# One fused transformer layer with a PEER expert stage: order of the three split matmuls, number of split buffers, and place of the extra tokens' rows

## The chip, the cores and the metric

The kernel runs on one core of a Trainium2 chip. The metric is device time in microseconds of one execution; lower is better. The engines are TensorE (PE, with its weight loads PEld), VectorE (DVE), ScalarE (ACT), GpSimd (POOL) and SyncE (SP); most transfers are issued from SP's queue, gathers from POOL's.

## The reference

One layer for 512 tokens of width 2048, in float32:

```
h = rmsnorm(x) * (1 + sc1) + sh1                      # sc, sh, g from c_act @ ada_w + ada_b
x = x + g1 * (concat(MLA attention(h), gated linear attention(h)) @ w_out)
h = rmsnorm(x) * (1 + sc2) + sh2
x = x + g2 * peer(h);   out = rmsnorm(x)

peer(h): q = h @ w_q; scores against 2 x 128 sub-keys for each of 8 heads
         top 16 of each half, top 16 of their 256 sums -> 128 experts a token, of 16384
         gate = softmax(best scores)
         act  = gelu(h . u[expert]);   y = sum(gate * act * v[expert])
```

The last part decides the time: 512 tokens times 128 experts, each with a row of u and a row of v of 2048 floats.

## The kernel before

**Split matmuls.** A float32 product is made of three faster ones. `split` (L109) casts a weight tile to a rounded part `whi` on ACT (L112) and subtracts, `wlo = raw - whi`, on DVE or POOL (L113). `mm3` (L104) then issues, for each piece of 128 rows, high weights by high data (L105), high by low (L106) and low weights by high data (L107), one right behind the other:

```
mm(o, wh, xh, start=first, stop=False)
mm(o, wh, xl, start=False, stop=False)
mm(o, wl, xh, start=False, stop=last)
```

`load_w` (L260) fetches a raw tile of 512 KB (`wraw`, a ring of three, on SP) and splits it. `whi` and `wlo` have two buffers each, in the pool `ws`.

**Two ways for the experts.** 160 tokens, 128 and 32 "extra" ones, go the sparse way: their 128 experts' rows are gathered by index on POOL (`gat`, L956), DVE takes the dot with the token's row (`h2s`, or `h2sb` for the extra tokens, L962), applies gelu and gate, and adds weighted rows of v to `acc0` or `accb` (L972). The rows h2s and h2sb are made by `hc` copies on ACT (L885), matmuls with the identity and copies out (L889), all ahead of the gate generation.

The other 352 tokens go the dense way, over all 16384 experts. `product1(j)` (L811) is h times u for 128 experts: two tiles of 24 matmuls each into one bank `p1`, then Gelu (L820) into `wt`. `gate` (L1010) multiplies `wt` with the dense gate tile `gtile` (L1017) and splits it (L1020, L1021). `product2(pair, g)` (L1025) is one tile of v, 256 experts by 512 columns: split (L1030 ACT, L1031 DVE) and 24 matmuls, the three of `mm3` in one bank before the next bank. Four column groups g share six banks `p2`; at a group's end `evacuate` adds its four banks to `xo` (L1046, DVE).

**Order.** Chunks of 4 or 6 j's run through the four groups; steps alternate: an odd step draws the next product1 (two tiles) ahead of its product2, an even step draws one step of the late modulation (`advance`, L279; DVE multiply and add L227 on a raw tile from the same ring of `wraw`). Sparse steps are strewn in between. Every engine's instructions run in a fixed order, which the tile framework's scheduler works out from the program's order and the buffers.

**Ahead of the dense stage.** After the retrieval (DVE), `NPRE` = 8 product1 are placed in the program ahead of the gate softmax (exp L839, ACT), with the low parts made on POOL. Then come slots and rows, the gate generation (L905 to L930: one-hot tiles on DVE L912, L913, L917, 704 matmuls L924, evictions `stg` on ACT L927, a transfer to DRAM), and more product1 until `RAW` = 12 beyond the `NHOST` = 8 in `xo` are stored; then product2 begins.

Of the kernel before, what the change touches and what calls it, by code (L numbers as in the profile page):

```python
# [9 lines left out]
F32 = mybir.dt.float32  # L10
F32R = mybir.dt.float32r
# [5 lines left out]
OP = mybir.AluOpType  # L17
AX = mybir.AxisListType
PSUM = bass.MemoryType.PSUM
LEFT, RIGHT = "left", "right"  # L20

P = 128
T = 512
TB = 4
D = 2048
KD = 16
# [9 lines left out]
NT = T - NA  # L36
GT = 32
# [12 lines left out]
SEQ = "A0 G0 A1 B0 G1 A2 B1 G2 A3 B2 G3 A4 B3 F8-12 A5 B4 A6 F0-4 B5 A7 B6 F4-7 B7 F7-8"  # L50
EWAIT = 2
KBLOCKS = ((0, 3), (3, 3), (6, 3), (9, 4), (13, 3))
RAW = 12
NPRE = 8
NLO = 5
NLAT = 6
LOWEST = -3.4028235e38
# [27 lines left out]
def hybrid_layer(ctx, tc, a, out):  # L85
# [13 lines left out]
    def bank(tag):  # L99
        return cur[tag][0].tile([P, 512], F32, name="b_" + tag, tag=tag)  # L100
# [3 lines left out]
    def mm3(o, wh, wl, xh, xl, first, last):  # L104
# [3 lines that stand above are left out]
# [556 lines left out]
    gate0 = keep.tile([P, P], F32, name="gate0")  # L664
    eidxb = keep.tile([P, NB], U32, name="eidxb")
    gateb = keep.tile([P, NB], F32, name="gateb")
    ws = pools.push("ws", LEFT, bufs=2)
    korder = list(range(8, 16)) + list(range(8))
    mhi, mlo = {}, {}
    for i, pieces in enumerate((((mhi, korder[:8]), (mlo, korder[:NLO])),  # L670
# [140 lines left out]
    def product1(j, lo_eng):  # L811
        b = bank("p1")
        b3 = b[:, :NT].rearrange("p (a b) -> p a b", a=NQ)
        wt = xo[:, j if j < DG else KD - NHOST + j, :] if j < NHOST else upl.tile([P, NT], F32, name="wt", tag="wt")
        for k0 in range(0, KD, 8):
            uh, ul = load_w(ws, a["u_t"][j][:, k0:k0 + 8, :], [P, 8, P], lo_eng)
            for kk in range(8):
                k = k0 + kk
                mm3(b3, uh[:, kk, :], ul[:, kk, :], h2[0][:, GA:, k, :], h2[1][:, GA:, k, :], k == 0, k == KD - 1)
        nc.scalar.activation(wt, b[:, :NT], AF.Gelu)  # L820
        raw[j] = wt

# [49 lines left out]
    nc.vector.tensor_tensor(out=slot[:, 3], in0=gres, in1=slot[:, 2], op=OP.subtract)  # L872
    pools.pop("retr")
    hsp = pools.push("h2s", RIGHT)
    h2s = hsp.tile([P, D], F32, name="h2s")
    h2sb = hsp.tile([P, D], F32, name="h2sb")
    hcp = pools.push("hcp", RIGHT, bufs=2)
    for dst, g0 in ((h2s, 0), (h2sb, GA - 1)):
        for k4 in range(4):
            b = bank("pj")  # L880
            ks = slice(k4 * 4, (k4 + 1) * 4)
            for n, src in enumerate(h2):
                hc = hcp.tile([P, 4, P // GT, GT], F32R, name="hc", tag=f"hc{n}")
                x = src[:, 0:P // GT, ks, :] if g0 == 0 else src[:, g0:g0 + 1, ks, :].broadcast_to([P, QB, 4, NB])
                nc.scalar.copy(out=hc, in_=x.rearrange("p g k t -> p k g t"))  # L885
                for j in range(4):
                    mm(b[:, j * P:(j + 1) * P], hc[:, j].rearrange("p g t -> p (g t)"), identr,
                       start=(j == 0 and n == 0), stop=(j == 3 and n == 1))
            nc.scalar.copy(out=dst[:, k4 * 512:(k4 + 1) * 512], in_=b)  # L889
    pools.pop("hcp")  # L890
    psum_done("pj", "sk", "m")
    psum(gg=6)

# [39 lines left out]


    sp = pools.push("sparse", RIGHT, bufs=3)
    acc0 = sp.tile([P, D], F32, name="acc0", bufs=1)
    accb = sp.tile([P, D], F32, name="accb", bufs=1)
    act0 = sp.tile([P, NA], F32, name="act0", bufs=1)
    wt0 = sp.tile([P, NA], F32, name="wt0", bufs=1)
    nc.gpsimd.memset(acc0, 0.0)  # L940
    nc.gpsimd.memset(accb, 0.0)

    pace = [None, None]
# [2 lines left out]
    def after(ins, name, cls):  # L946
        if name is not None:
            tc.add_manual_dep(ins.ins, name, mybir.DependencyInfo(cls, mybir.DependencyReason.DATA), reason="pace")
# [20 lines left out]

    def add(s, g):  # L970
        acc = of(s, acc0, accb)[0]
        after(nc.vector.scalar_tensor_tensor(out=acc, in0=g, scalar=wt0[:, s:s + 1], in1=acc,  # L972
                                             op0=OP.mult, op1=OP.add), pace[1], ORDER)

    LAG = 2

# [48 lines left out]
    def product2(pair, g, banks, first, last):  # L1025
        vr = ws.tile([P, 2, 512], F32, name="wraw", tag="wraw", bufs=NWRAW)
        nc.sync.dma_start(out=vr, in_=a["v_t"][pair][g])
        vh = ws.tile([P, 2, 512], F32R, name="whi", tag="whi")
        vl = ws.tile([P, 2, 512], F32R, name="wlo", tag="wlo")
        pace[0] = nc.scalar.copy(out=vh, in_=vr).ins.name  # L1030
        pace[1] = nc.vector.tensor_tensor(out=vl, in0=vr, in1=vh, op=OP.subtract).ins.name  # L1031
        for jj in range(2):
            wh, wl = wpair[pair * 2 + jj]
            for dc in range(DG):
                dsl = slice(dc * P, (dc + 1) * P)
                mm3(banks[dc][:, :NT], vh[:, jj, dsl], vl[:, jj, dsl], wh, wl, first and jj == 0, last and jj == 1)

    fresh = [True] * DG

# [25 lines left out]
        nc.sync.dma_start(out=g2d[:, c0:c0 + width], in_=acc[0:1, :])  # L1065

    def onto_x1(g):
        x1t = fin.tile([P, DG, NT], F32, name="x1t", tag="x1t")
        nc.sync.dma_start(out=x1t, in_=x1f[:, g * DG:(g + 1) * DG, :])
        for dc in range(DG):  # L1070
            n = g * DG + dc
            nc.vector.scalar_tensor_tensor(out=xo[:, n, :], in0=xo[:, n, :], scalar=G2[:, n:n + 1], in1=x1t[:, dc, :],
                                           op0=OP.mult, op1=OP.add)
# [182 lines left out]
```

## Time and profile before

| | |
|---|---|
| median of 3 runs | 3469.57 us (3462.45 to 3469.78) |
| profiled execution, its own time | 3448.51 us |
| its span in the trace | 3446.6 us |
| PE busy | 3133.1 us, 91% of the span, mean granted clock 0.967 |
| DVE busy | 2574.2 us, 75% |
| ACT busy | 1143.7 us, 33% |
| POOL busy | 980.1 us, 28% |
| DMA | 849.26 MB, mean 246 GB/s |

The shares are means over stages of different kinds; the dense stage, from about 1335 us on, is three fifths of the span. Busy time of PE counts matmuls as the trace records them; they overlap, so the sum of durations is more than the time between starts. A wait row tells who waited and for which engine's line. "PEclk" in a window is the clock that TensorE was granted, as a share of full speed.

### The profile page before, as it was taken

What the parts mean: (1) busy time and instruction counts of PE and PEld (TensorE: products, weight loads), DVE (VectorE), ACT (ScalarE), POOL (GpSimd) and SP (SyncE); (2) the same over time, 40 slices, a digit from 0 to 9 for tenths busy, and PEclk for the clock granted to TensorE, in tenths of its full rate; (3) what the DMA queues carried; (4) which work ended last, traced back from release to release, by engine and by line L of the source; (5) the groups of instructions that cost most, each with busy time, mean ns of one, the idle gap of its engine ahead of it and who ended that gap; (6) DMA issues with size and microseconds to landing.
All of it is one profiled execution on the core that took longest, in us unless ns stands there. A gap on an engine that the chain in (4) does not pass through costs nothing. (4 is left out here: it accounts for less than half of the span.)

```text
span 3446.6 us, 45915 instructions
## 1 busy us (share of the span) xinstructions
PE 3133.1 (91%) x17569; PEld 2864.9 (83%) x17569; DVE 2574.2 (75%) x3632; ACT 1143.7 (33%) x1594; POOL 980.1 (28%) x631
## 2 busy tenths in 40 slices
PE   3999999999997889989999899899989989899998
PEld 2777776787776878989999898898989889899997
DVE  8988936774897495777777777777877677777776
ACT  3333453423222674222222222222222222222333
POOL 5454511111444444222222221222222222222210
PEclk9999999999998999999999999999999999999999
DMA  7876710283222358888888888887988788787874
GB/s 225 266 249 218 254 59 19 91 288 128 92 86 80 135 214 294 319 302 316 319 315 318 302 292 305 304 302 286 332 299 305 280 302 301 288 303 291 331 278 168
DMA packets 266652, 849.26 MB, mean 246 GB/s; under 512 B 25560, under 2 KB 97912, under 8 KB 222688
## 3 DMA queue, kind: packets, MB, share of 16 engines
q1 hardware_dynamic: 219840, 510.66, 44.3%
q0 software_dynamic: 46592, 335.68, 24.6%
q8 instruction: 137, 2.24, 0.3%
q14 instruction: 83, 0.68, 0.1%
HBM read 814.74 MB, written 31.47 MB: 246 GB/s over the span
## 5 line engine op out<-in xcount | busy, mean ns | idle before, releaser
L107 PE MATMUL b_p<-h2hi,wlo 128*128 128x352 f32 x4096 | 1372.6, 336 | 164.5 <-DVE wlo L113 144.4
L105 PE MATMUL b_p<-h2hi,whi 128*128 128x352 f32 x4096 | 1362.4, 333 | 28.8 <-ACT whi L112 23.2
L106 PE MATMUL b_p<-h2lo,whi 128*128 128x352 f32 x4096 | 1355.7, 331 | 0.0
L107 PEld LDWEIGHTS b_p<-h2hi,wlo 128*128 128x128 f32 x4096 | 793.4, 194 | 192.2 <-DVE wlo L113 166.8
L105 PEld LDWEIGHTS b_p<-h2hi,whi 128*128 128x128 f32 x4096 | 794.1, 194 | 36.8 <-ACT whi L112 23.9
L106 PEld LDWEIGHTS b_p<-h2lo,whi 128*128 128x128 f32 x4096 | 793.2, 194 | 0.1
L112 ACT CAST whi<-wraw 128x1024 fp32r<-128x1024 f32 (+2 forms) x459 | 414.3, 905 | 968.2 <-PE b_p L106 440.2
L1030 ACT CAST whi<-wraw 128x1024 fp32r<-128x1024 f32 x256 | 268.8, 1050 | 918.7 <-PE b_p L106 839.1
L1031 DVE TENSOR_TENSOR wlo<-wraw,whi 128x1024 fp32r<-128x1024 f32 x256 | 313.2, 1223 | 303.8 <-ACT whi L1030 303.4
L113 POOL TENSOR_TENSOR wlo<-wraw,whi 128x512 fp32r<-128x512 f32 (+3 forms) x211 | 404.5, 1924 | 472.3 <-ACT whi L112 442.8
L956 POOL DMA_INDIRECT gat<-in_u_rows,eidx x128 | 195.4, 1527 | 614.1 <-ACT whi L1030 479.1
L956 POOL DMA_INDIRECT gat<-in_v_rows,eidx x128 | 185.6, 1450 | 612.9 <-ACT whi L1030 451.0
L227 DVE SCALAR_TENSOR_TENSOR acc<-adaw,cact,acc 128x512 f32<-128x512 f32 (+1 forms) x330 | 305.5, 948 | 26.4 <-DMA adaw<-in_ada_w 21.5
L113 DVE TENSOR_TENSOR wlo<-wraw,whi 128x1024 fp32r<-128x1024 f32 x248 | 298.2, 1217 | 31.0 <-ACT whi L112 30.2
L972 DVE SCALAR_TENSOR_TENSOR acc<-gat,wt,acc 128x2048 f32<-128x2048 f32 x128 | 300.3, 2346 | 20.1 <-DMA gat<-in_v_rows,eidx 19.9
L962 DVE SCALAR_TENSOR_TENSOR gat<-gat,h2s 128x2048 f32<-128x2048 f32 x128 | 291.7, 2286 | 25.6 <-DMA gat<-in_u_rows,eidx 25.3
L227 DVE SCALAR_TENSOR_TENSOR acc<-wraw,cact,acc 128x512 f32<-128x512 f32 x60 | 45.1, 751 | 148.4 <-DMA wraw<-in_ada_w 148.4
L1046 DVE TENSOR_TENSOR xo<-b_p,xo 128x352 f32<-128x352 f32 x236 | 106.9, 514 | 0.2 <-PE b_p L107 0.2
L107 PE MATMUL b_pj<-h2hi,wlo 128*128 128x512 f32 x256 | 102.4, 401 | 3.6 <-POOL wlo L113 3.6
L105 PE MATMUL b_pj<-h2hi,whi 128*128 128x512 f32 x256 | 102.8, 403 | 2.8 <-ACT h2hi L724 2.1
L106 PE MATMUL b_pj<-h2lo,whi 128*128 128x512 f32 x256 | 103.2, 404 | 2.0 <-DVE h2lo L725 2.0
L927 ACT ACTIVATE stg<-b_gg 128x512 f32<-128x512 f32 x88 | 87.2, 1131 | 43.3 <-PE b_gg L924 30.1
(368 smaller groups left out, 3786.0 us busy)
## 6 DMA issues: line engine op xcount, KB each, us to landing
wraw<-in_u_t SPq DMA_DIRECT2D x256, 512.0 KB, 4.7
wraw<-in_v_t SPq DMA_DIRECT2D x256, 512.0 KB, 4.8
adaw<-in_ada_w SPq DMA_DIRECT2D x224, 256.0 KB, 4.5
adaw<-in_ada_w SPq DMA_DIRECT2D x128, 192.0 KB, 3.5
gd<-stg SPq DMA_DIRECT2D x11, 2048.0 KB, 9.4
gtile<-gd SPq DMA_DIRECT2D x32, 704.0 KB, 6.6
wraw<-in_w_out SPq DMA_DIRECT2D x32, 512.0 KB, 4.5
wraw<-in_w_q SPq DMA_DIRECT2D x32, 512.0 KB, 3.6
```

The source lines that it names most:

```text
L105: mm(o, wh, xh, start=first, stop=False)
L106: mm(o, wh, xl, start=False, stop=False)
L107: mm(o, wl, xh, start=False, stop=last)
L112: nc.scalar.copy(out=hi, in_=src)
L113: (nc.vector if lo_eng == "vector" else nc.gpsimd).tensor_tensor(out=lo, in0=src, in1=hi, op=OP.subtract)
L227: nc.vector.scalar_tensor_tensor(out=acc, in0=w[:, j, :], scalar=cact[:, k:k + 1], in1=acc, op0=OP.mult, op1=OP.add)
L956: ins = nc.gpsimd.indirect_dma_start(out=g, out_offset=None, in_=a[table], in_offset=bass.IndirectOffsetOnAxis(ap=idx[:, c:c + 1], axis=0))
L962: after(nc.vector.scalar_tensor_tensor(out=g, in0=g, scalar=1.0, in1=of(s, h2s, h2sb)[0], op0=OP.mult, op1=OP.mult, accum_out=act0[:, s:s ...
L972: after(nc.vector.scalar_tensor_tensor(out=acc, in0=g, scalar=wt0[:, s:s + 1], in1=acc, op0=OP.mult, op1=OP.add), pace[1], ORDER)
L1030: pace[0] = nc.scalar.copy(out=vh, in_=vr).ins.name
L1031: pace[1] = nc.vector.tensor_tensor(out=vl, in0=vr, in1=vh, op=OP.subtract).ins.name
L1046: nc.vector.tensor_tensor(out=o, in0=banks[dc][:, :NT], in1=o, op=OP.add)
```

## The change

1. In product1 and product2 the matmuls of a tile are written in another order: first all 16 with the high weights, then the 8 with the low weights.
2. The pool `ws` gets three buffers instead of two for `whi` and `wlo`; `wraw` stays at three.
3. `RAW` goes from 12 to 13 and `NPRE` from 8 to 11, so three more product1 stand in the program ahead of the gate softmax.
4. The pool of the `hc` tiles is gone; they take turns in `whi` and `wlo`. The rows of the extra tokens, h2sb, are made ahead of the gate generation, the rows h2s after it, in banks of `p2`.
5. `acc0` is the tile h2sb, free after the extra tokens' dots; its zeroing is dropped, and the first addition is a multiplication that writes.
6. `x1t` at the end takes turns with `gtile`.

```
-RAW = 12
-NPRE = 8
+RAW = 13
+NPRE = 11
...
-    ws = pools.push("ws", LEFT, bufs=2)
+    ws = pools.push("ws", LEFT, bufs=3)
...
             for kk in range(8):
-                k = k0 + kk
-                mm3(b3, uh[:, kk, :], ul[:, kk, :], h2[0][:, GA:, k, :], h2[1][:, GA:, k, :], k == 0, k == KD - 1)
+                for x in h2:
+                    mm(b3, uh[:, kk, :], x[:, GA:, k0 + kk, :], start=k0 + kk == 0 and x is h2[0], stop=False)
+            for kk in range(8):
+                mm(b3, ul[:, kk, :], h2[0][:, GA:, k0 + kk, :], start=False, stop=k0 + kk == KD - 1)
...
-    h2s = hsp.tile([P, D], F32, name="h2s")
     h2sb = hsp.tile([P, D], F32, name="h2sb")
-    hcp = pools.push("hcp", RIGHT, bufs=2)
-    for dst, g0 in ((h2s, 0), (h2sb, GA - 1)):
+
+    def to_rows(dst, g0, ps):
         for k4 in range(4):
-            b = bank("pj")
+            b = bank(ps)
...
-                hc = hcp.tile([P, 4, P // GT, GT], F32R, name="hc", tag=f"hc{n}")
+                hc = ws.tile([P, 4, P // GT, GT], F32R, name="hc", tag=("whi", "wlo")[n])
...
-    pools.pop("hcp")
+    to_rows(h2sb, GA - 1, "pj")
     psum_done("pj", "sk", "m")
...
-    acc0 = sp.tile([P, D], F32, name="acc0", bufs=1)
+    acc0 = h2sb
+    h2s = sp.tile([P, D], F32, name="h2s", bufs=1)
+    to_rows(h2s, 0, "p2")
...
-    nc.gpsimd.memset(acc0, 0.0)
...
+        if s == 0:
+            ins = nc.vector.tensor_scalar(out=acc, in0=g, scalar1=wt0[:, s:s + 1], scalar2=None, op0=OP.mult)
...
-        for jj in range(2):
-            wh, wl = wpair[pair * 2 + jj]
-            for dc in range(DG):
-                dsl = slice(dc * P, (dc + 1) * P)
-                mm3(banks[dc][:, :NT], vh[:, jj, dsl], vl[:, jj, dsl], wh, wl, first and jj == 0, last and jj == 1)
+        for part in (vh, vl):
+            for jj in range(2):
+                for dc in range(DG):
+                    for x in wpair[pair * 2 + jj][:2 if part is vh else 1]:
+                        mm(banks[dc][:, :NT], part[:, jj, dc * P:(dc + 1) * P], x,
+                           start=first and jj == 0 and part is vh and x is wpair[pair * 2 + jj][0],
+                           stop=last and jj == 1 and part is vl)
...
-        x1t = fin.tile([P, DG, NT], F32, name="x1t", tag="x1t")
+        x1t = sp.tile([P, DG, NT], F32, name="x1t", tag="gtile", bufs=2)
```

The change moves instructions in every engine's order. Three places follow, each of before and then of the changed kernel. Line numbers of the changed kernel are up to 8 higher: product2's cast and subtraction are L1036 and L1037, the four additions L1054.

DVE at the end of a column group behind which an even step follows, with the modulation (L227); L113 are the low parts of product1 tiles, L962 or L964 the dots, L1017 or L1023 the gate multiplication. Before:

```order
L1031 TENSOR_TENSOR wlo_15534<-wraw_15531,whi_15533 128x1024
L962 SCALAR_TENSOR_TENSOR gat_15492,act0_10963<-gat_15492,h2s_9568 128x2048
L1046 TENSOR_TENSOR xo_7121<-b_p2_15389,xo_7121 128x352
L1046 TENSOR_TENSOR xo_7121<-b_p2_15390,xo_7121 128x352
L1046 TENSOR_TENSOR xo_7121<-b_p2_15391,xo_7121 128x352
L1046 TENSOR_TENSOR xo_7121<-b_p2_15392,xo_7121 128x352
L113 TENSOR_TENSOR wlo_15574<-wraw_15571,whi_15573 128x1024
L113 TENSOR_TENSOR wlo_15604<-wraw_15601,whi_15603 128x1024
L1017 TENSOR_TENSOR wt_15430<-wt_15430,gtile_15817 128x352
L227 SCALAR_TENSOR_TENSOR acc_14971<-wraw_15679,cact_87,acc_14971 128x512
```

And with the change:

```order
L964 SCALAR_TENSOR_TENSOR gat_15582,act0_11147<-gat_15582,h2s_11089 128x2048
L113 TENSOR_TENSOR wlo_15631<-wraw_15628,whi_15630 128x1024
L1023 TENSOR_TENSOR wt_15487<-wt_15487,gtile_15874 128x352
L113 TENSOR_TENSOR wlo_15661<-wraw_15658,whi_15660 128x1024
L227 SCALAR_TENSOR_TENSOR acc_15028<-wraw_15736,cact_87,acc_15028 128x512
L1054 TENSOR_TENSOR xo_7121<-b_p2_15446,xo_7121 128x352
L1054 TENSOR_TENSOR xo_7121<-b_p2_15447,xo_7121 128x352
L1054 TENSOR_TENSOR xo_7121<-b_p2_15448,xo_7121 128x352
L1054 TENSOR_TENSOR xo_7121<-b_p2_15449,xo_7121 128x352
L1037 TENSOR_TENSOR wlo_15698<-wraw_15695,whi_15697 128x1024
```

The low parts of two product1 tiles, the gate and the modulation have moved from behind the four additions to ahead of them.

DVE at the end of a group behind which product2 follows at once, of the next group. Before:

```order
L1031 TENSOR_TENSOR wlo_15399<-wraw_15396,whi_15398 128x1024
L962 SCALAR_TENSOR_TENSOR gat_15349,act0_10963<-gat_15349,h2s_9568 128x2048
L1046 TENSOR_TENSOR xo_7121<-b_p2_15147,xo_7121 128x352
L1046 TENSOR_TENSOR xo_7121<-b_p2_15148,xo_7121 128x352
L1046 TENSOR_TENSOR xo_7121<-b_p2_15149,xo_7121 128x352
L1046 TENSOR_TENSOR xo_7121<-b_p2_15150,xo_7121 128x352
```

And with the change:

```order
L1037 TENSOR_TENSOR wlo_15456<-wraw_15453,whi_15455 128x1024
L964 SCALAR_TENSOR_TENSOR gat_15406,act0_11147<-gat_15406,h2s_11089 128x2048
L964 SCALAR_TENSOR_TENSOR gat_15439,act0_11147<-gat_15439,h2s_11089 128x2048
L113 TENSOR_TENSOR wlo_15491<-wraw_15488,whi_15490 128x1024
L1023 TENSOR_TENSOR wt_15344<-wt_15344,gtile_15874 128x352
L1054 TENSOR_TENSOR xo_7121<-b_p2_15204,xo_7121 128x352
```

A second dot, a product1 tile's low part and a gate multiplication now stand between product2's low part and the additions.

ACT from the last rows ahead of the gate generation into it (`stg` is the eviction of one generation bank, `hc` the copies for the token rows, L112 the casts of product1's tiles). Before:

```order
L889 COPY h2sb<-b_pj 128x512 x2
L112 CAST whi<-wraw 128x1024
L927 ACTIVATE stg<-b_gg 128x4x128 x2
L112 CAST whi<-wraw 128x1024
L927 ACTIVATE stg<-b_gg 128x4x128 x2
L820 ACTIVATE wt<-b_p_10967 128x352
L927 ACTIVATE stg<-b_gg 128x4x128 x6
L112 CAST whi<-wraw 128x1024
```

And with the change:

```order
L886 COPY hc<-h2lo 128x512
L928 ACTIVATE stg<-b_gg 128x4x128 x88
L886 COPY hc<-h2hi 128x512
L886 COPY hc<-h2lo 128x512
L112 CAST whi<-wraw 128x1024 x3
L890 COPY h2s<-b_p_11090 128x512
```

All 88 evictions now stand in a row, and product1's casts, which were between them, behind them and behind the first `hc` copies for h2s. Further ahead in ACT's order the exp of the gate softmax stands behind two casts after the first Gelu, where it stood behind one.

## Rows read from the trace of the kernel before

**Rows 1.** Windows by stage: length, busy time of each engine (instructions), clock, DMA.

```profile
core 0: us, PE busy (x) PEld busy (x) DVE busy (x) ACT busy (x) POOL busy (x), PEclk, DMA share, GB/s
1070.00:1093.00 23.00, 0.03 (x1) 0.03 (x1) 22.90 (x106) 3.39 (x5) 0.00 (x0) 0.55 0.00 0
1162.00:1306.00 144.00, 118.86 (x1072) 103.35 (x1071) 128.31 (x167) 101.02 (x110) 66.88 (x16) 0.92 0.54 204
1335.00:2690.00 1355.00, 1249.63 (x7337) 1221.04 (x7338) 1016.60 (x1012) 387.88 (x480) 313.84 (x217) 0.97 0.85 308
2690.00:3300.00 610.00, 561.87 (x3328) 553.49 (x3328) 442.45 (x425) 173.30 (x210) 147.91 (x98) 0.97 0.81 300
1335.00:3397.00 2062.00, 1906.13 (x11251) 1868.41 (x11252) 1536.03 (x1523) 595.02 (x730) 472.86 (x321) 0.97 0.83 303
```

**Rows 2.** Windows of 20 us in the dense stage.

```profile
2980.00:3000.00 20.00, 16.28 (x88) 15.98 (x87) 13.61 (x15) 4.02 (x5) 4.21 (x3) 0.85 0.88 314
3060.00:3080.00 20.00, 20.00 (x126) 20.00 (x125) 13.81 (x12) 6.30 (x9) 5.28 (x3) 1.00 0.78 293
2760.00:2780.00 20.00, 16.86 (x105) 16.57 (x103) 16.31 (x19) 5.61 (x6) 4.53 (x3) 0.98 0.98 365
```

**Rows 3.** PE's groups by line, 1335:3397: busy us, mean ns, idle before, releasers.

```profile
L107 PE MATMUL b_p<-h2hi,wlo 128*128 128x352 f32 x3735 | 1245.6, 334 | 152.7 <-DVE wlo L113 144.4 <-DVE wlo L1031 5.4 <-POOL wlo L113 2.8
L105 PE MATMUL b_p<-h2hi,whi 128*128 128x352 f32 x3734 | 1237.5, 332 | 5.6 <-DVE xo L1046 5.4
```

**Rows 4.** Waits in the dense stage: us in total, times, longest.

```profile
PE b_p L107 <- DVE wlo L113: 144.4, 77, 4.4
```

**Rows 5.** Timeline 1902 to 1909, one end of a group: start, length.

```profile
1902.28 2.35 DVE L972 SCALAR_TENSOR_TENSOR acc<-gat,wt,acc 128x2048 f32<-128x2048 f32 x1 [0.41 <-DMA gat<-in_v_rows,eidx]
...
1904.17 1.05 ACT L112 CAST whi<-wraw 128x1024 fp32r<-128x1024 f32 x1 [1.04 <-PE b_p L106]
...
1904.55 1.81 DVE L1046 TENSOR_TENSOR xo<-b_p,xo 128x352 f32<-128x352 f32 x4
1906.27 2.35 DVE L113 TENSOR_TENSOR wlo<-wraw,whi 128x1024 fp32r<-128x1024 f32 x2
...
1907.54 0.43 PE L107 MATMUL b_p<-h2hi,wlo 128*128 128x352 f32 x1 [2.92 <-DVE wlo L113]
```

**Rows 6.** Waits of DVE in 1340 to 3390.

```profile
DVE acc L227 <- DMA wraw<-in_ada_w: 148.4, 58, 4.8
...
DVE gat L962 <- DMA gat<-in_u_rows,eidx: 25.3, 22, 2.6
```

**Rows 7.** DMA issues in 1340 to 3390: KB each, median us to landing.

```profile
wraw<-in_u_t SPq DMA_DIRECT2D x216, 512.0 KB, 4.8
...
wraw<-in_ada_w SPq DMA_DIRECT2D x64, 256.0 KB, 5.2
```

**Rows 8.** Waits of the whole program around the gate softmax.

```profile
ACT gates L839 <- DVE gates L838: 25.4, 1, 25.4
PE b_p L105 <- ACT whi L112: 23.2, 1, 23.2
```

**Rows 9.** Window of the gate generation, product1's matmuls alone: PE, PEld, DVE, ACT.

```profile
1162.00:1306.00 144.00, 87.13 (x368) 63.02 (x367) 0.00 (x0) 4.01 (x8) 0.92 0.54 204
```

**Rows 10.** Timelines of DVE and POOL in the gate generation.

```profile
1178.77 0.68 DVE L912 TENSOR_TENSOR o<-iota,slot 128x1024 f16<-128x1024 f16 x1
1179.37 1.28 DVE L917 TENSOR_TENSOR o<-o,slot 128x1024 f16<-128x1024 f16 x2
...
1208.33 2.87 DVE L912 TENSOR_TENSOR o<-iota,slot 128x1024 f16<-128x1024 f16 x1
...
1206.23 4.42 POOL L113 TENSOR_TENSOR wlo<-wraw,whi 128x1024 fp32r<-128x1024 f32 x1 [6.80 <-PE b_gg L924]
```

**Rows 11.** Groups of the page and by line: busy us, mean ns, idle before.

```profile
L927 ACT ACTIVATE stg<-b_gg 128x512 f32<-128x512 f32 x88 | 87.2, 1131 | 43.3 <-PE b_gg L924 30.1
...
L693 PE MATMUL b_o<-mixpart,whi 128*128 128x512 f32 x256 | 64.9, 393 | 0.0
```

More of the change, by code (lines that the diff above doesn't have):

```diff
@@ L971, in add @@
         acc = of(s, acc0, accb)[0]
-        after(nc.vector.scalar_tensor_tensor(out=acc, in0=g, scalar=wt0[:, s:s + 1], in1=acc,
-                                             op0=OP.mult, op1=OP.add), pace[1], ORDER)
+        if s == 0:
+            ins = nc.vector.tensor_scalar(out=acc, in0=g, scalar1=wt0[:, s:s + 1], scalar2=None, op0=OP.mult)
+        else:
+            ins = nc.vector.scalar_tensor_tensor(out=acc, in0=g, scalar=wt0[:, s:s + 1], in1=acc,
+                                                 op0=OP.mult, op1=OP.add)
+        after(ins, pace[1], ORDER)
     LAG = 2
```

## The prediction

> **What bounds the kernel now.** I read the windows by stage first. The dense expert stage, 1335 to 3397, is 2062 of 3446.6 us; in it PE is busy 1906 us at a granted clock of 0.97, DVE 1536, DMA 0.83 [rows 1]. So PE is the bound there and nothing else is full. Next, what PE's pace would be unhindered. A quiet window of 20 us, 3060 to 3080, has 126 matmuls at clock 1.00 [rows 2], 0.159 us each; I take 0.160. A matmul's own 0.33 us [rows 3] is no pace, since two overlap. The stage's 11,251 matmuls at 0.160 us would take 1800 us, so 262 us are lost.
>
> The groups of PE show where: 152.7 us idle ahead of the matmul with the weights' low part, 144.4 of it on DVE's subtraction L113, the low part of a product1 tile [rows 3], in 77 waits of up to 4.4 us [rows 4]. The other 100 us are mostly time at half clock: a disturbed window, 2980 to 3000, has 88 matmuls at clock 0.85 [rows 2], 38 fewer than the quiet one, and the granted clock falls after the longer waits.
>
> The timeline at 1904 shows why [rows 5]. When a group of product2 ends, DVE adds its four banks to the result (L1046, 1.81 us) and only then makes the low parts (2.35 us for two). PE meets the tile's first low part at its third matmul, 0.32 us in, and stands 2.92 us.
>
> **The change part by part.** The profiled execution took 3448.5 us, 0.6% less than the median of 3469.6; I sum against the former and carry the difference to the latter. I count in chunks of 24 tiles (576 matmuls, 92.2 us at 0.160). In 1335 to 2690, where the modulation (L227) still runs, 7337 matmuls in 1355 us [rows 1] make 12.74 chunks of 106.4 us; in 2690 to 3300, 3328 in 610 us make 5.78 of 105.6.
>
> *Low parts last, third buffer pair.* PE now reaches a tile's first low part after 16 matmuls, 2.6 us, instead of 2. The third whi/wlo pair lets DVE make the next product1 tile's low part ahead of the evacuation; the order of DVE's instructions shows that at both kinds of group end. Together these cover the 2.92 us of the timeline, and waits of 1.88 us on average (144.4/77). So the L113 wait and the half-clock time go, but not down to PE's pace, because of what is late next: DVE. In the first part DVE is busy 1016.6 of 1355 us [rows 1], 79.8 us a chunk. It also stands on data: L227 waits 148.4 us in 58 times for its own DMA, 2.56 each [rows 6], and that stays, since its wraw slot is freed by DVE itself a few instructions earlier and the transfer needs 5.2 us to land [rows 7]. Over 12.74 chunks that is 11.6 us each; waits for gathered rows (25.3 in all for the dot, [rows 6], and about as much for the add) are 2.6 over the 19.3 chunks of the stage. DVE thus needs 94.0 us a chunk, PE 92.2. Neither can get far ahead of the other, so what holds one up still holds up the other. I leave half of today's 14.2 us above PE's floor and take 99: 12.74 x (106.4 - 99) = 94 us gained. The ends: 92.2 (DVE's waits hidden after all) gives 181, 106.4 gives 0. In the second part DVE needs 442.45/610 x 105.6 = 76.6 us a chunk and PE binds alone; I leave 3.3 us above the floor for the bank waits below: 5.78 x (105.6 - 95.5) = 58 us, ends 77 and 0. Sum 152.
>
> *Evacuation later.* Its price is what the change adds: the four additions now stand behind the next product1 tile's low part (1.2 us), the gate multiplication and, at one kind of end, the modulation's wait. Queued behind them is product2's fifth matmul, which needs a freed bank: a group holds 4 of 6. The row of today is 5.4 us in all (L105 on DVE L1046, [rows 3]). From below it costs nothing, since DVE gets there earlier and one or two product1 tiles of 3.84 us run first at one kind of end; from above see the last rival. The 3.3 us a chunk (three ends, 1.1 us each) is nearer to the row.
>
> *Product2's low parts* now go from bank to bank at every matmul, where three in a row stayed in one. The quiet window has a bank change at every third matmul, 126 in 20 us at clock 1.00 [rows 2]: no room for a cost, so I take none. The Trainium skill's "TensorE: Matmul & The Clock Gate", section "HAM oscillation", reports a bf16 kernel whose cycling through PSUM banks idled the engine often enough for the clock to swing; it speaks against this edit, the quiet window here against the rule. By the row the term is 0, by the rule it would cost the 328 us of (d).
>
> *Gate softmax later, three more product1 tiles ahead of it.* Today ACT stands 25.4 us at the exp for DVE's gates, and PE waits 23.2 us behind it for a cast [rows 8]; in 1070 to 1093 PE is idle [rows 1]. In ACT's new order the exp comes after two casts behind the first Gelu, not one. So one more product1 tile half (24 matmuls, 3.8 us) fits in; most of the hole stays, as the other tiles' casts are still behind the exp. I count PE as resuming at 1093 with 8 tiles to go: 8 x 48 x 0.160 = 61.4, till 1154.
>
> *Rows of h2s after the gate generation, hc from the whi/wlo buffers.* This is where the change loses. The order shows 88 stg evictions in a row on ACT: the hc copies for h2s wait for PSUM that is free only after the generation, and as they take turns in whi/wlo, product1's casts queue behind them. Today 368 product1 matmuls run in 1162 to 1306 beside the generation [rows 9], 59 us at 0.160. After: the extra tokens' rows and slots take about 6 us, till 1161. The generation alone is bound by DVE: 176 instructions. Undisturbed they start 0.60 us apart; beside a POOL subtraction of 4.42 us one took 2.87 [rows 10]. With POOL's subtractions gone I take 176 x 0.60 = 106 us plus 3 to start, till 1270; ACT's 88 x 1.13 = 99 us [rows 11] fits beside. Ends: 106, or 144 as now [rows 1]. Then rows of h2s, 4 us, and the other 10 tiles of 21: 480 x 0.160 = 76.8, till 1351. Today product2 starts at 1335 with 20 tiles done, one fewer (7.7 us). So 16 - 8 = +8 us, ends +8 and +46.
>
> *The rest.* In PE's new order the last 16 matmuls of the output projection's first heads (L693), which filled gaps of the attention, stand behind it: at most 16 x 0.39 us [rows 11] = 6.3, at least 0; I take 3. The dropped memset, the shared acc0 and the first addition as a plain multiplication (2.3 us of DVE either way) and x1t from gtile's buffers move no bound: nothing for them.
>
> **Sum:** -94 - 58 + 8 + 3 = -141 us; 3448.5 gives 3307 for a profiled execution, and 3469.6 gives **3329 us** for the median.
>
> **The rivals.**
> (a) *DVE's waits are hidden too.* With DVE ahead, L227's transfer could land while PE works off tiles that are ready. For it: in the new order the low parts of two product1 tiles are made ahead of L227. Against it: the transfer is issued only when DVE frees its slot, and 94.0 is above 92.2. Then PE's floor holds: 12.74 x 14.2 + 5.78 x 13.4 = 258 gained, less 11: 3223; band 3223 to 3290.
> (b) *The ring of three wraw slots binds.* It stays at three, with five loads for four tiles in the first part. A slot is held 4.8 us for landing [rows 7], 1.05 for the cast, 1.2 for the subtraction, and what DVE does ahead: one dot (2.35) gives 9.4, an evacuation more 11.2. Over 3 slots, times 5/4, times 24 tiles this is 94 to 112 us a chunk; the middle, 103, gains 43. If the second part also gets half, 29, less 11, the time is 3409; band 3375 to 3440. For it: DMA stands at 0.83 and would rise to 0.89; a window with 365 GB/s is at DMA 0.98 with 105 matmuls only [rows 2]. Against it: ACT's casts wait mostly for PE today, not for DMA.
> (c) *Evacuations hold PE (slower).* At a group end on an odd step product2 follows at once, and covers only its first 4 matmuls, 0.64 us. DVE stands ahead of the banks with one more dot (2.35), a low part (1.2) and a gate (0.5, by its size one of the four additions): 4.1 us. At the other kind of end it is the modulation's 2.56. At full price, 32 x 4.1 + 31 x 2.56 = 210 us over 63 ends: 3539. It makes the kernel slower from 141/63 = 2.2 us a group end on. Against it: each stall of PE lets DVE catch up, and today's banks wait 5.4 us in all.
> (d) *Bank changes cost clock (slower).* If product2's low parts ran at half clock: 256 x 8 x 0.160 = 328 us more, 3657. The quiet window speaks against it. The Trainium skill's rule named above would make this the outcome.
> (e) *The edits don't reach the order,* and what pays is eaten by the generation at 144 us and the longer product1 tail: within 0.2% of 3470.
>
> **How the numbers follow.** Forecast, 3290 to 3375: 0.55. (a) 0.13, (b) 0.16, a smaller gain still, 3440 to 3461: 0.04. (e) 0.04. Slower 0.08: (c) 0.07, (d) 0.01. A measurement of this kernel can tell about 0.2% from no change. Faster 0.55 + 0.13 + 0.16 + 0.04 = 0.88. The range 3240 to 3440 leaves out some 0.04 of (a) below, and the smaller gain, (e) and the slower cases, 0.16, above.
>
> **What would show it.** Right: PE's wait on DVE's product1 low parts falls from 144 us to under 40; the dense stage's granted clock rises to 0.99; a chunk takes 99 us in the first part and 95.5 later; L227 still waits about 2.5 us each time; in the generation no product1 matmul stands beside it, its DVE instructions last under 0.7 us, and product2 starts near 1351. Wrong: product2's high matmuls waiting on DVE's evacuation for over 100 us (c); ACT's casts waiting for wraw's DMA for more than today (b); no DVE-bound stretch, chunks at 93 (a); a clock near 0.5 in product2's low parts (d).

## The result: 2.6% faster, two thirds of the forecast gain

The changed kernel takes 3380.1 us (median of 4 runs, 3365.5 to 3386.0) against 3469.7 before; the ratio is 0.974, 95% interval 0.971 to 0.978. The forecast was 3329, within 3240 to 3440. The measured time is within that range, but 5 us above the band that the forecast itself got, 3290 to 3375, and in that of rival (b), 3375 to 3440. The two profiled executions differ by less than the medians, 3381.0 against 3446.6 us of span, since that of before lay 21 us below its median and that of after 3 above.

First the windows by stage of the changed kernel (length, busy time and instructions of each engine, clock, DMA share, GB/s), to be read beside [rows 1]:

```profile
core 0: us, PE busy (x) PEld busy (x) DVE busy (x) ACT busy (x) POOL busy (x), PEclk, DMA share, GB/s
1181.00:1288.00 107.00, 75.00 (x690) 63.08 (x688) 100.85 (x166) 81.38 (x86) 0.00 (x0) 0.65 0.47 197
1370.00:2690.00 1320.00, 1219.53 (x7294) 1202.88 (x7292) 1006.49 (x1000) 378.61 (x475) 361.97 (x215) 0.96 0.87 313
2690.00:3250.00 560.00, 553.05 (x3400) 549.68 (x3400) 455.40 (x440) 179.34 (x217) 149.97 (x100) 1.00 0.92 337
```

A chunk of 576 matmuls now takes 1320 x 576/7294 = 104.2 us while the late modulation runs (before 106.4) and 560 x 576/3400 = 94.9 us after it (before 105.6). The second part is at PE's pace, clock 1.00. The first has hardly moved, at clock 0.96.

Next the waits of 1340 to 3330 (total us, times, longest), to be read beside [rows 3, 4, 6]:

```profile
ACT whi L1036 <- DMA wraw<-in_v_t: 521.6, 104, 12.5
...
ACT whi L112 <- DMA wraw<-in_u_t: 182.4, 90, 4.8
DVE acc L227 <- DMA wraw<-in_ada_w: 158.0, 50, 6.2
...
PE b_p L1042 <- DVE xo L1054: 86.3, 19, 7.0
...
PE b_p L821 <- DVE wlo L113: 0.9, 1, 0.9
```

Of PE's 144.4 us behind product1's low parts, 0.9 are left (one wait). In their place PE waits 86.3 us for the banks that the four additions free. And ACT's casts, which waited for PE before, now wait for wraw's transfers: 704 us in all, where it was 115. The rows of before, in the same stretch:

```profile
ACT whi L1030 <- PE b_p L106: 795.5, 208, 10.1
ACT whi L112 <- PE b_p L106: 411.2, 189, 4.6
...
ACT whi L112 <- DMA wraw<-in_u_t: 68.6, 18, 5.5
...
ACT whi L1030 <- DMA wraw<-in_v_t: 46.8, 14, 4.7
```

Where the bank waits come from is to be seen at 1473 to 1498, a stretch that recurs about once a chunk (timeline of ACT, DVE, PE and SP's queue: start, length):

```profile
1480.62 0.33 SPq L1033 DMA_DIRECT2D wraw<-in_v_t  x1
1481.62 0.75 DVE L227 SCALAR_TENSOR_TENSOR acc<-wraw,cact,acc 128x512 f32<-128x512 f32 x1 [1.03 <-DMA wraw<-in_ada_w]
1482.40 0.33 SPq L262 DMA_DIRECT2D wraw<-in_u_t  x1
...
1488.31 1.04 ACT L1036 CAST whi<-wraw 128x1024 fp32r<-128x1024 f32 x1 [8.71 <-DMA wraw<-in_v_t]
1489.39 1.23 DVE L1037 TENSOR_TENSOR wlo<-wraw,whi 128x1024 fp32r<-128x1024 f32 x1 [3.18 <-ACT whi L1036]
1490.53 4.73 DVE L977 SCALAR_TENSOR_TENSOR accb<-gat,wt,accb 128x2048 f32<-128x2048 f32 x2
1490.64 0.33 SPq L1033 DMA_DIRECT2D wraw<-in_v_t  x1
...
1495.18 1.22 DVE L113 TENSOR_TENSOR wlo<-wraw,whi 128x1024 fp32r<-128x1024 f32 x1
1496.32 0.52 DVE L1023 TENSOR_TENSOR wt<-wt,gtile 128x352 f32<-128x352 f32 x1
1496.75 1.81 DVE L1054 TENSOR_TENSOR xo<-b_p,xo 128x352 f32<-128x352 f32 x4
1497.32 0.66 PE L1042 MATMUL b_p<-h2hi,whi 128*128 128x352 f32 x1 [6.99 <-DVE xo L1054]
```

A load is issued when DVE has finished with a slot: 1482.40 at the end of L227, 1490.64 at the end of L1037. The tile issued at 1480.62 is cast at 1488.31, 7.7 us later. DVE waits for that cast, then runs two sparse additions, a low part and a gate, and only then adds the four banks. PE stands 6.99 us. DVE's steps are the ones that rival (c) named, with one sparse step more. That they are late because the load was is so far only read from this stretch; the run with four slots below tests it.

### The profile page after: what moved, and what is told of

It reads as the page before. It is cut to its first block, busy times and chain, and to the rows that moved or that the text cites. A ratio compares the mean times of both kernels' runs of the same rounds, so it can differ in the third digit from the quotient of the medians.

```text
span 3381.0 us, 46005 instructions
## 1 busy us (share of the span) xinstructions
PE 3111.1 (92%) x17569; PEld 2862.1 (85%) x17569; DVE 2552.5 (75%) x3630; ACT 1138.3 (34%) x1594; POOL 999.7 (30%) x632
## 5 line engine op out<-in xcount | busy, mean ns | idle before, releaser
L1042 PE MATMUL b_p<-h2hi,whi 128*128 128x352 f32 x2048 | 675.6, 332 | 105.5 <-DVE xo L1054 86.3
L112 ACT CAST whi<-wraw 128x1024 fp32r<-128x1024 f32 (+2 forms) x459 | 413.7, 904 | 886.9 <-DMA wraw<-in_u_t 196.6
L819 PE MATMUL b_p<-h2hi,whi 128*128 128x352 f32 x2048 | 671.0, 328 | 21.8 <-ACT xo L822 21.4
L1042 PE MATMUL b_p<-h2lo,whi 128*128 128x352 f32 x2048 | 668.8, 329 | 0.0
L819 PE MATMUL b_p<-h2lo,whi 128*128 128x352 f32 x2048 | 667.3, 326 | 0.0
L1036 ACT CAST whi<-wraw 128x1024 fp32r<-128x1024 f32 x256 | 268.7, 1050 | 967.2 <-DMA wraw<-in_v_t 521.6
L113 POOL TENSOR_TENSOR wlo<-wraw,whi 128x512 fp32r<-128x512 f32 (+3 forms) x213 | 378.3, 1784 | 524.9 <-ACT whi L112 352.9
L1042 PEld LDWEIGHTS b_p<-h2hi,whi 128*128 128x128 f32 x2048 | 395.9, 193 | 120.2 <-DVE xo L1054 92.7
L1037 DVE TENSOR_TENSOR wlo<-wraw,whi 128x1024 fp32r<-128x1024 f32 x256 | 312.7, 1223 | 198.9 <-ACT whi L1036 153.5
L819 PEld LDWEIGHTS b_p<-h2hi,whi 128*128 128x128 f32 x2048 | 386.7, 189 | 22.7 <-ACT xo L822 21.7
L1042 PEld LDWEIGHTS b_p<-h2lo,whi 128*128 128x128 f32 x2048 | 397.1, 194 | 0.0
L819 PEld LDWEIGHTS b_p<-h2lo,whi 128*128 128x128 f32 x2048 | 386.6, 189 | 0.1
L1042 PE MATMUL b_p<-h2hi,wlo 128*128 128x352 f32 x2048 | 376.8, 326 | 1.2 <-DVE wlo L1037 0.6
L821 PE MATMUL b_p<-h2hi,wlo 128*128 128x352 f32 x2048 | 376.0, 326 | 1.6 <-DVE wlo L113 0.9
L958 POOL DMA_INDIRECT gat<-in_u_rows,eidx x128 | 211.6, 1654 | 547.3 <-ACT whi L1036 329.5
L958 POOL DMA_INDIRECT gat<-in_v_rows,eidx x128 | 204.8, 1600 | 554.4 <-ACT whi L1036 363.3
L1042 PEld LDWEIGHTS b_p<-h2hi,wlo 128*128 128x128 f32 x2048 | 340.7, 191 | 3.0 <-DVE wlo L1037 2.9
L821 PEld LDWEIGHTS b_p<-h2hi,wlo 128*128 128x128 f32 x2048 | 340.1, 188 | 2.5 <-DVE wlo L113 1.6
L113 DVE TENSOR_TENSOR wlo<-wraw,whi 128x1024 fp32r<-128x1024 f32 x246 | 300.0, 1220 | 45.2 <-ACT whi L112 41.5
L227 DVE SCALAR_TENSOR_TENSOR acc<-adaw,cact,acc 128x512 f32<-128x512 f32 (+1 forms) x330 | 310.7, 964 | 21.5 <-DMA adaw<-in_ada_w 16.8
L977 DVE SCALAR_TENSOR_TENSOR h2sb<-gat,wt,h2sb 128x2048 f32<-128x2048 f32 x127 | 298.1, 2347 | 12.6 <-DMA gat<-in_v_rows,eidx 11.8
L964 DVE SCALAR_TENSOR_TENSOR gat<-gat,h2s 128x2048 f32<-128x2048 f32 x128 | 290.8, 2286 | 17.8 <-DMA gat<-in_u_rows,eidx 16.2
```

Source lines behind the costliest of these rows:

```text
L112: nc.scalar.copy(out=hi, in_=src)
L113: (nc.vector if lo_eng == "vector" else nc.gpsimd).tensor_tensor(out=lo, in0=src, in1=hi, op=OP.subtract)
L227: nc.vector.scalar_tensor_tensor(out=acc, in0=w[:, j, :], scalar=cact[:, k:k + 1], in1=acc, op0=OP.mult, op1=OP.add)
L819: mm(b3, uh[:, kk, :], x[:, GA:, k0 + kk, :], start=k0 + kk == 0 and x is h2[0], stop=False)
L821: mm(b3, ul[:, kk, :], h2[0][:, GA:, k0 + kk, :], start=False, stop=k0 + kk == KD - 1)
L958: ins = nc.gpsimd.indirect_dma_start(out=g, out_offset=None, in_=a[table], in_offset=bass.IndirectOffsetOnAxis(ap=idx[:, c:c + 1], axis=0))
```

## The experiments

The ratio of each row is to runs of before on the same chip in the same session (before: 3458 to 3467 us there). A chunk is 576 x length / PE's matmuls in the windows 1400 to 2700 (the modulation runs) and 2700 to 3200 (it is over). The windows are fixed, so in a faster kernel the modulation ends inside the first: its last step at L227 stands at 2644 in the changed kernel, but at 2511 in four_wraw, 2440 in ada_own_slot and 2390 in ada_two_slots.

| kernel | median us | ratio to before (95%) | chunk, first part | chunk, second part |
|---|---|---|---|---|
| before | 3469.7 | 1 | 106.9 | 106.4 |
| changed | 3380.1 | 0.974 (0.971 to 0.978) | 104.6 | 93.9 |
| two_buffers | 3389.1 | 0.979 (0.976 to 0.982) | 104.9 | 94.4 |
| old_order_three | 3394.9 | 0.982 (0.979 to 0.985) | 106.0 | 93.9 |
| before_four_wraw | 3436.0 | 0.995 (0.993 to 0.997) | 105.4 | 105.0 |
| ada_own_slot | 3318.2 | 0.958 (0.955 to 0.961) | 98.8 | 94.6 |
| ada_two_slots | 3303.0 | 0.953 (0.949 to 0.956) | 97.2 | 94.5 |
| no_late_modulation | 3268.8 | 0.944 (0.941 to 0.947) | 95.8 | 93.2 |
| four_wraw | 3272.7 | 0.946 (0.943 to 0.949) | 95.8 | 93.4 |
| old_order_four | 3290.4 | 0.952 (0.949 to 0.955) | 97.1 | 93.3 |
| rows_own_buffer | 3374.1 | 0.973 (0.971 to 0.976) | 106.6 | 93.4 |
| four_wraw_rows | 3283.2 | 0.951 (0.947 to 0.954) | 98.4 | 93.9 |
| two_pairs_five_wraw | 3375.2 | 0.977 (0.974 to 0.981) | 107.1 | 93.1 |
| additions_first | 3427.5 | 0.990 (0.987 to 0.993) | 104.3 | 103.4 |

**Which half of the change brought the gain?** The order without the third pair, and the third pair without the order.

```
-    ws = pools.push("ws", LEFT, bufs=3)
+    ws = pools.push("ws", LEFT, bufs=2)
```

is two_buffers; old_order_three puts the lines with `mm3` of before back into product1 and product2 and leaves the rest as changed.

> The changed kernel with two whi/wlo buffers instead of three: the new order of the matmuls without the third pair. In DVE's order the four additions then stand ahead of the next product1's low part again at one kind of group end. Theory: the order alone takes the waits for low parts away (2.6 us of cover), and the third pair does little or even costs, since it is what puts the additions late: 3350 to 3385, and PE's 7 us waits for the additions shrink. Rival: the third pair is needed to make low parts ahead, and without it waits of 1 to 2 us for low parts return at 77 places, with their time at half clock: 3420 to 3470.

> The changed kernel with the three matmuls of each piece in a row again, as before; three pairs of buffers and all else as changed: the third pair without the new order. Theory (the order does it, the pair adds little): PE's waits for the low parts of product1 stay above 80 us, and 22 us of later start of product2 remain: 3440 to 3490, no faster than before. Rival (the pair lets DVE make low parts ahead of the additions, and this is the gain): waits under 40 us, 3390 to 3410.

Either alone brings the second part to 94 us a chunk. Alone they are worth 2.1% and 1.8%, together 2.6%: they take away the same waits. For two_buffers the time is 4 us above the band of its theory and far from that of its rival; PE's waits for the additions shrank, to 35.1 us. The theory for old_order_three fell, and its rival was right. PE's waits in it (1370 to 3250):

```profile
PE b_p L105 <- DVE xo L1050: 46.1, 12, 4.2
PE b_p L107 <- DVE wlo L113: 32.3, 25, 4.2
PE b_p L107 <- DVE wlo L1035: 18.7, 21, 2.2
```

The waits for product1's low parts are 32.3 us with the old order of the matmuls, where before has 140.2 in that stretch, since DVE makes the low part ahead of the additions. Neither alone nor both move the first part: 104.6 to 106.0 beside 106.9. No run takes the other parts of the change alone, save the place of the rows (below).

**What holds the first part?** Four runs take away what the modulation adds, or give it room.

In ada_own_slot, with RAW 12 (ada_two_slots has bufs=2 and RAW 11):

```
-            return ws.tile([P, 512], F32, name="wraw", tag="wraw", bufs=NWRAW)
+            return sp.tile([P, 512], F32, name="adaw2", tag="adaw2", bufs=1)
```

In four_wraw:

```
-NWRAW = 3
+NWRAW = 4
...
-RAW = 13
+RAW = 10
```

In no_late_modulation:

```
-        for k0 in range(0, KD, kn):
+        for k0 in range(0, 1 if pool is ws else KD, kn):
```

> The changed kernel, but the late modulation's tiles come from a buffer of their own (one, 2 KB a partition) instead of the ring of three wraw slots; RAW 12 instead of 13 to make room. Theory R (the ring of wraw slots, with five loads for four tiles, is what binds while the modulation runs): the chunk of 576 matmuls there falls from 104.3 us to 95 or 96, as in the later part; over 12.7 chunks that is 105 to 118 us, so about 3270. Rival E (once a chunk the four additions stand behind two sparse additions, a low part and a gate on DVE, and that holds PE 7 us whatever the ring does): chunks stay at 104, time 3370 to 3390. Rival D (DVE's own load binds): 99 a chunk, about 3313.

> The changed kernel with 15 of 16 pieces of the late modulation (the last of the six sections) left out, transfers and DVE work both; the output is then not the reference's. It bounds from below what the modulation costs. Theory R: the chunk in the first part falls to 95, as in the second, the 7 us waits of PE for the four additions go: 12.7 x 9.3 = 118 less, about 3262. Rival E: chunks at 102 to 104 with a 7 us wait once a chunk, about 3370.

> As the run with one buffer of its own for the late modulation, but with two (RAW 11 to make room). With one, L227 still waited 88.8 us for its transfer, up to 8.0 at a time, with the four additions queued behind it (PE's waits for them up to 9.8). Theory: the transfer is issued too late because it shares SP's queue with loads that wait for wraw slots; with two buffers it is issued a step earlier, the waits of L227 fall under 25 us, PE's long waits for the additions go, a chunk of the first part takes 95 or 96: 3275 to 3295. Rival: DVE's load in the first part is what is left (99 a chunk): 3318 within 10.

> The changed kernel with a ring of four wraw slots instead of three, the modulation's tiles still in it (RAW 10 to make room). If it is the number of slots that binds, five loads for four tiles now have a third more slots: chunks of the first part at 95 to 98, 3275 to 3310, ACT's waits for wraw's transfers far shorter. If it is only that L227's transfer starts late, behind DVE's own low parts, chunks fall to 99 or 100 only: about 3325. If neither, 3380.

With 15 of 16 pieces of the modulation left out the first part runs at 95.8 us a chunk; with four slots and the modulation in, at the same 95.8. In 1440 to 2390, where the modulation runs in every kernel that has it, it is 96.7 and 96.4, beside 104.1 with the change, 99.3 in ada_own_slot and 98.2 in ada_two_slots. So neither DVE's work nor the traffic of the modulation is what costs, but the slots: five loads for four tiles in a ring of three. The windows of four_wraw, and its waits in 1370 to 3250:

```profile
1400.00:2700.00 1300.00, 1277.17 (x7815) 1265.92 (x7814) 1081.11 (x1071) 410.81 (x497) 330.99 (x230) 0.99 0.93 341
2700.00:3200.00 500.00, 498.69 (x3084) 497.50 (x3083) 407.73 (x407) 165.06 (x199) 107.48 (x78) 1.00 0.89 325
```

```profile
PE b_p L1042 <- DVE xo L1054: 24.1, 13, 5.7
...
ACT whi L1036 <- DMA wraw<-in_v_t: 93.4, 24, 7.1
ACT whi L112 <- DMA wraw<-in_u_t: 39.2, 14, 5.4
```

DMA moves 341 GB/s there, where it moved 313: bandwidth was not the limit. ACT's waits for wraw fall from about 700 to 133 us, and PE's bank waits from 86 to 24, though in DVE's order the additions still stand behind two sparse steps, a low part and a gate or a modulation step (these two have changed places). That settles the bank waits as a consequence of late loads. `RAW` was lowered for room in these runs, and no run lowers it alone; but no_late_modulation keeps 13 and comes to the same chunk, and before_four_wraw (below), with 11 for 12, moves little. A slot of its own for the modulation brings less. Its 98.8 us a chunk and 3318 us are what its rival D (DVE's own load binds) had said, 99 and 3313; but in four_wraw DVE has the same work a chunk, 79.7 us against 79.3, and a chunk takes 95.8, so DVE's load is not what bound. What the trace of ada_own_slot shows is that DVE meets its transfer at L227 before it has landed, with the additions behind it. Waits of ada_own_slot, then of ada_two_slots (1370 to 3250):

```profile
PE b_p L1042 <- DVE xo L1054: 54.9, 16, 9.8
...
DVE acc L227 <- DMA adaw<-in_ada_w: 88.8, 33, 8.0
```

```profile
PE b_p L1042 <- DVE xo L1054: 43.0, 14, 12.3
...
DVE acc L227 <- DMA adaw<-in_ada_w: 31.7, 13, 9.6
```

The second buffer took 57 us of waits at L227 but only 15 us of time; the expectation of 3275 to 3295 was missed by 8 us, and PE's long waits for the additions did not go.

**Was the ring the bound before, too?** One slot more on the kernel before (with x1t in gtile's buffers and RAW 11 for room).

```
-NWRAW = 3
+NWRAW = 4
```

> The kernel before with one thing changed: a ring of four wraw slots instead of three (to make room RAW 11 instead of 12, and x1t in gtile's buffers as in the change). If before was held only by the low parts that DVE makes behind the four additions, the slot more does nothing: the second part stays at 105.6 us a chunk, PE waits over 100 us for low parts, 3440 to 3470. If the ring already held the first part before, that part falls to 97 to 100 and the second stays: 12.7 x 7 = 89 less, about 3380.

It brings 0.5%, 4 us more than the first theory allowed, and neither part moves by more than 1.5 us a chunk. The reason stands in PE's first row of waits (1370 to 3250): the waits for low parts are all there. DVE's wait at L227 is nearly gone, 13.3 us where it was 148.4, and that alone gave almost nothing.

```profile
PE b_p L107 <- DVE wlo L113: 139.3, 78, 5.1
...
DVE acc L227 <- DMA wraw<-in_ada_w: 13.3, 8, 4.2
```

So before, low parts held both parts. The change took them away, and in the first part the ring of slots stood right behind, 2 us a chunk lower.

**Is the order worth more once the ring does not bind?** Four slots and three pairs as above, with the `mm3` lines of before.

> The run with four wraw slots (3273 us), with the three matmuls of each piece in a row again as before; three pairs of buffers. It asks what the new order is worth once the ring does not bind. If little, as with three slots (15 us): 3280 to 3300. If the ring hid its worth in the first part: PE's waits for low parts of 50 us and more there, with half-clock time, 3320 to 3360.

Its 3290 against 3273 with the new order: 0.6%, the intervals do not overlap. Low parts cost 22.4 us of waits in it, 14 times. It is as little as with three slots.

**Slots instead of pairs.** Hc in gathered rows' buffers (below), and

```
-NWRAW = 3
+NWRAW = 5
...
-    ws = pools.push("ws", LEFT, bufs=3)
+    ws = pools.push("ws", LEFT, bufs=2)
```

> The same space spent otherwise: two whi/wlo pairs, five wraw slots, RAW 13, hc copies of h2s in gathered rows' buffers, the new order of the matmuls. If slots of wraw are worth more than a third pair at any count: 3235 to 3250. If four slots are enough and the third pair then counts (two pairs cost 9 us with three slots): 3255 to 3275.

Both expectations fell: 3375, and a chunk of 107.1 in the first part. Five slots with two pairs are hardly better than three with two (3389); four slots with three pairs are 107 us better than three with three. Casts no longer wait for transfers but for PE and DVE to free a pair, and DVE for the modulation (1400 to 2700):

```profile
ACT whi L1039 <- PE b_p L819: 369.8, 126, 5.8
ACT whi L112 <- PE b_p L1045: 356.4, 118, 15.3
...
DVE acc L227 <- DMA wraw<-in_ada_w: 266.3, 55, 10.4
...
PE b_p L1045 <- DVE xo L1057: 68.5, 12, 10.8
ACT whi L112 <- DVE wlo L1040: 56.9, 13, 8.2
```

A tile can be ahead only if it has both a slot and a pair. Why L227 waits 266 us in this kernel, with more slots than any other, can be read from a stretch of its timeline (DVE and SP's queue):

```profile
2041.30 1.26 DVE L1040 TENSOR_TENSOR wlo<-wraw,whi 128x1024 fp32r<-128x1024 f32 x1 [0.94 <-ACT whi L1039]
...
2042.49 2.34 DVE L980 SCALAR_TENSOR_TENSOR h2sb<-gat,wt,h2sb 128x2048 f32<-128x2048 f32 x1
2042.59 0.33 SPq L221 DMA_DIRECT2D wraw<-in_ada_w  x1
...
2049.61 0.75 DVE L227 SCALAR_TENSOR_TENSOR acc<-wraw,cact,acc 128x512 f32<-128x512 f32 x1 [4.79 <-DMA wraw<-in_ada_w]
```

The modulation's load is issued when a low part has freed a slot, and in DVE's order only one sparse addition stands between that and L227. In four_wraw two low parts of product1 tiles stand between as well (2012 to 2019, where L227 does not wait). That this order comes from the missing pair was not tested.

**The four additions first.** DVE's order with the additions ahead of the next product1's low part and of the step's sparse work.

In `split` the low part is ordered behind the last addition, and after `evacuate` the sparse work is:

```
+        if lo_eng == "vector" and emptied[0] is not None:
+            tc.add_manual_dep(sub.ins, emptied[0], mybir.DependencyInfo(mybir.DependencyClass.NoSync, mybir.DependencyReason.DATA), reason="pace")
...
+                emptied[0] = nc.vector.tensor_tensor(out=o, in0=banks[dc][:, :NT], in1=o, op=OP.add).ins.name
...
                 evacuate(g, banks)
+                if emptied[0] is not None:
+                    pace[1] = emptied[0]
+                sparse_some(PER2)
```

> The changed kernel, but in DVE's order the four additions at a group's end stand ahead of the next product1's low part and of the sparse work of that step. Rival E: PE's waits for the additions (86 us) fall under 20, with the half-clock time behind them, and the time to 3290 to 3320. Theory R: the additions were only late because the ring was late; PE waits for product2's cast or low part instead, chunks stay at 101 to 104: 3350 to 3380.

Neither: it is 1.6% slower than the changed kernel, and loses in the second part, 103.4 instead of 93.9. Two rows of its waits (1370 to 3250):

```profile
DVE xo L1058 <- PE b_p L1046: 119.0, 36, 6.2
...
ACT whi L112 <- DMA wraw<-in_u_t: 350.6, 164, 7.4
```

DVE now stands at the additions until PE has finished the group, and the low parts behind them, which free wraw's slots, come late: casts of u tiles wait 350.6 us instead of 182.4. With three slots the late additions of the changed kernel are the better order; with four this was not tried.

**The empty gate generation.** hc of h2s in the gathered rows' buffers, so that product1's casts do not queue behind it; then the same with four slots.

```
-                hc = ws.tile([P, 4, P // GT, GT], F32R, name="hc", tag=("whi", "wlo")[n])
+                if ps == "pj":
+                    hc = ws.tile([P, 4, P // GT, GT], F32R, name="hc", tag=("whi", "wlo")[n])
+                else:
+                    hc = sp.tile([P, D], F32R, name="hc", tag="gat")[:, :512].rearrange("p (k g t) -> p k g t", k=4, t=GT)
```

> The changed kernel, but the hc copies for the rows of h2s take buffers of the gathered rows instead of whi/wlo, so that product1's casts no longer queue behind them; in ACT's order product1 then stands between the evictions of the gate generation again. If the empty generation is what costs the 22 us by which product2 starts later than before (1363 against 1341 at equal matmul counts), then product1's matmuls run beside the generation, which gets longer by POOL's subtractions (107 to about 140 us), and product2 starts 15 to 20 us earlier: about 3362. Rival: what the filled generation gains, its lengthening gives back: 3380 within 7.

> Four wraw slots (RAW 11) and the hc copies of h2s in gathered rows' buffers, so that product1 fills the gate generation. With three slots the 21 us that the rows' own buffer gained ahead of product2 were lost again in the first part, where chunks took 106 instead of 104. If the ring took them back, they stay now: 3273 - 21, about 3252. If the filled generation costs them elsewhere, 3273 within 7.

In the generation product1's matmuls are back; window 1181 to 1288 of rows_own_buffer, beside the first window of after above:

```profile
1181.00:1288.00 107.00, 89.29 (x817) 78.16 (x815) 103.75 (x134) 76.83 (x85) 56.78 (x11) 0.92 0.56 212
```

DVE makes 134 instead of 166 instructions in it, PE 817 instead of 690 matmuls. Product2 starts at 1342.9 instead of 1370.9; 7 of the 28 us lie ahead of product1 already. So the first half of the theory held, 21 us, but the end comes hardly earlier: 3374 is within the interval of the changed kernel, as the rival had it, and 3283 is 10 us above four_wraw, where neither expectation put it. The first part's chunk is 2.0 us longer with three slots and 2.6 with four, 25 and 32 us over 12.4 chunks (four_wraw_rows has `RAW` 11, four_wraw 10). That it was the ring which took the gain back is refuted by the second run. What does, stays open.

## Why the prediction was right in sign and range, and 51 us short

That the time lies within the range is owed to the room that the range left for rival (b): the forecast's own mechanism holds for the second part of the dense stage, that of (b) for the first.

- **The bound, right.** Low parts held PE, and their waits are gone, 144.4 us to 0.9. The half-clock time went in the second part, clock 1.00; in the first the bank waits took their place, clock 0.96. So the dense stage's 0.99 that the prediction named did not come: 0.97 in 1340 to 3330.
- **The second part, right.** 58 us forecast (95.5 a chunk), (105.6 - 94.9) x 5.78 = 62 measured.
- **The first part, the step that failed.** 94 us forecast (99 a chunk), (106.4 - 104.2) x 12.7 = 28 measured. The step passed the bound from PE to DVE at 94.0 us a chunk. DVE's own sum was right: 1006.5 us busy and 158 at L227 over 12.66 chunks are 92.0, and the gathers add about 2. But DVE was not what came late next. The ring of three slots was, as rival (b) had it: 103 a chunk there, 104.2 measured, and four slots give 95.8. Rival (b) was given 0.16 because ACT's casts waited for PE, not for DMA, in the trace of before. That argument does not hold, and the sign that the prediction named for (b), more of ACT's waits for wraw's transfers, came, 115 us to 704: while PE stands for something else, the transfers have time to land, and the row says nothing of what they will do at PE's new pace. Its own working, 9.4 to 11.2 us a slot, was the better evidence.
- **L227's wait stays, right,** and is longer: 158.0/50 = 3.2 us each instead of 2.56.
- **The bank waits of rival (c)** came to 86.3 us, nearly all in the first part; four slots bring them to 24, so they follow from (b).
- **Ahead of product2, 8 us forecast, 22.6 measured.** Product2 starts at 1370.9 where 1351 was forecast. The generation went nearly as forecast: no product1 or POOL work beside it in 1181 to 1288, the DVE instructions at 0.68 us. Product1's first matmul starts 10 us later:

```profile
1058.96 0.33 PE L819 MATMUL b_p<-h2hi,whi 128*128 128x352 f32 x1
```

  It stands at 1048.81 in before. In ada_own_slot, whose program is the changed one up to there, it stands at 1047.28, and in the other runs between 1049 and 1060. So the 10 us are spread between executions, and neither the 3 us forecast for the attention nor their absence can be read from them. The other 10 us of the 20 are small pieces. On the shifted start the generation was due at 1171; its first DVE instruction stands at 1174.1 and its last matmul at 1287.0, 113 us later for a forecast of 109, and product2 follows after 84 us for 81.

```profile
1174.11 0.69 DVE L913 TENSOR_TENSOR o<-iota,slot 128x1024 f16<-128x1024 f16 x1
```

  On the other side product2's start of before was taken 5.6 us too early: its first matmul there, the 961st of the dense products, is at 1340.6, not 1335.
- **The exp, right.** ACT waits 25.68 us there now, 25.4 before [rows 8]; the later place in the program moved it by one cast:

```profile
1102.77 0.63 ACT L841 ACTIVATE gates<-gates 128x512 f32<-128x512 f32 x1 [25.68 <-DVE gates L840]
```

- **Bank changes cost nothing, right.** Product2's low parts change bank at every matmul, and the second part has 3400 matmuls in 560 us, 0.165 us each, at clock 1.00; old_order_three, with three matmuls in a row in one bank, takes the same 93.9 us a chunk there (2700 to 3200) as the changed kernel. What the Trainium skill's "TensorE: Matmul & The Clock Gate", section "A second HAM failure mode: psum-queue depth-cycling" (it stands right behind the one that the prediction names), reports of bank cycling does not show here.

In the sum of the profiled spans: -28 - 62 + 22.6 = -67, measured -65.6. Against the forecast of -141 that is 75 us short: 66 in the first part and 15 ahead of product2, less 4 that the second part gave more.

## What to carry to other kernels

When a wait is taken away, ask what every buffer of the chain will do at the new pace, not whether its transfers wait at the old one: a slot's time from issue to release, times the loads per tile, over the number of slots, against the tile's time. A tile is ahead only if it has all its buffers, the raw slot and the split pair, so that one more of either alone may bring nothing and one of each much: here, in the new order, three slots with two pairs are 2.1% faster than before, three slots with three pairs 2.6%, five slots with two pairs 2.3%, four slots with three pairs 5.4%. Putting an engine's urgent work first in its order is no gain if the engine then stands waiting for it with other work behind.

## What was not expected of the hardware

A 512 KB load that landed in 4.8 us (median) before [rows 7] took 7.7 us from issue to cast at 1480, with three loads, a gate tile and gathers in flight; DMA's busy share in 1480 to 1500 was 0.97. In four_wraw the median landing of such a load was 6.3 us (u) and 6.8 us (v) in 1400 to 2390, with DMA moving 341 GB/s. So a ring sized by the landing time of a calmer trace can be too short for a faster one. And the start of the same stage differed by 12 us between two executions of programs that are alike up to there (1047.28 and 1058.96), more than several of the terms that the forecast worked out.

```profile
1480.00:1500.00 20.00, 10.93 (x59) 10.34 (x58) 15.45 (x15) 3.50 (x4) 5.92 (x3) 0.78 0.97 350
```
